# Transposes, splits and index matmuls of a mixture-of-experts stage, moved into the products before them

## The chip, the cores and the metric

One core of a Trainium2 chip runs the whole program. The metric is the time of one execution on the device, in microseconds; the number for a kernel is the median of its runs. Profiles come from one execution taken by the hardware profiler.

## What is computed

The reference is two blocks over 1024 tokens of 1024 channels. The first has a Fourier branch, a bidirectional mLSTM branch and a mixture of 16 experts, in which each expert chooses its 128 best tokens; the second is a hybrid mixer. The change touches the experts alone:

```python
aff = jax.nn.softmax(h @ w_router, axis=-1)
vals, idx = lax.top_k(jnp.swapaxes(aff, 1, 2), 128)
xs = h[idx]
hid = jax.nn.silu(xs @ w_gate) * (xs @ w_up)
y = (hid @ w_down) * vals[..., None]
x = x + ga2 * jnp.zeros_like(h).at[idx].add(y)
```

All weights are float32, 1024 x 1024 for each of the three products of an expert, and each is read once from device memory.

## The kernel before, in words

Matrix products are made in a fast reduced float format. To keep float32 accuracy, each operand is split into a high part (a copy in that format) and a low part (the rest); a product is then three matmuls, high by high, high by low and low by high (`mm3`, line 354).

**Weights.** Weights are loaded in units of 1 MB, two steps of 128 input channels each, on SyncE's queue. Each step is split: ScalarE copies the high part, VectorE subtracts to get the low part (`_split`, line 234). `prefetch` (line 263) keeps up to six split steps, five ahead of the one in use, and fills all other free memory with raw units. Memory is 25 slots of 8 KB a partition; a raw unit, a split step, an expert's tokens and a transposed operand take one slot each. `slot` (line 182) gives out the free slot that is done with first, by a plan of the engines' times that the kernel keeps while it is built; a load or a write into a slot waits until the slot's last use has ended.

**One expert.** The tokens of expert e are gathered by POOL from device memory by a list of indices (`gather`, line 1670), 128 tokens on partitions. `transp` (line 1676) turns them: TensorE transposes eight 128 x 128 blocks into two banks of PSUM, ScalarE copies the high part and VectorE subtracts for the low part. `prod` (line 1690) makes one product of 128 x 1024: 8 steps of 2 halves of 3 matmuls, 48 in all, over two banks. Gate goes through SiLU on ScalarE, is multiplied by up on VectorE, turned by `transp` again, and multiplied by down. VectorE scales the result and POOL adds it to the tokens in device memory with an indirect scatter.

**Indices.** `index` (line 1657) finds the tokens of an expert: one row of a 48-row table of running counts is spread over 128 partitions by a matmul with a one-hot column (two matmuls of 48 rows, one for each half of the 1024 tokens), and VectorE counts, over each half, how many running counts are not above its slot number. The table is filled once, before the first expert.

**Order.** The instructions are issued in an order written out by hand. Round e of the loop (line 1727) is: up of e; multiply by the gate of e; transpose the tokens of e+1; gather e+2; build the indices 2e+3 and 2e+4 (so that all are there after e = 6); gate of e+1, and its SiLU; transpose the hidden values of e; down of e; scale; scatter. Each engine works off its own instructions in this order. There are four PSUM banks for products (`pm`) and four for all else (`pa`). All instructions pass through one helper, so that the profile gives line 67 for each.

Of the kernel before, what the change touches and what calls it, by code (L numbers as in the profile page):

```python
# [9 lines left out]
FT = mybir.dt.float32  # L10
# [19 lines left out]
# columns of the host-laid-out vector tile  # L30
C_C, C_CC, C_G1, C_G2, C_GF, C_BA = 0, 8, 16, 24, 32, 40
C_WC = 56                 # 9 taps x 8 blocks
C_CA = C_WC + 72          # 3 taps x 2
C_DW = C_CA + 6           # 31 taps x 2
# [5 lines left out]
# constant table columns  # L40
# [13 lines left out]
class Queue:  # L54
    """an engine of the core that books what is given to it in the plan"""
# [15 lines left out]
class Plan:  # L71
    """the core with its engines, and about when each of them gets to what it has been given, in microseconds:
    background work is given to an engine when its operands are about to be there"""
# [79 lines left out]
class Kern:  # L153
# [27 lines left out]
    # ---- memory  # L181
    def slot(self, dt=FT, name="t"):
        """8 KB a partition"""
        s = Slot()
        assert self.free_slots, "out of slots: " + " ".join(sorted(x.c for x in self.live.values()))
        s.i, s.c = self.free_slots.pop(self.pick()), name
        self.live[s.i] = s
        self.n += 1
        s.t = self.sp.tile([128, SLOT], dt, tag=f"s{s.i}", name=f"{name}_{self.n}")
        self.tags[s.i] = s.t.tensor.tag  # L190
        return s

    def pick(self):
        """the slot that is done with first"""
        def at(i):
            tag = self.tags.get(i)
            return max((d[tag, b][0] for d in (self.nc.wrote, self.nc.read) for b in range(17) if (tag, b) in d), default=0.0)
        f = [at(i) for i in self.free_slots]
        return f.index(min(f))
# [14 lines left out]
    # ---- weights: raw units of 8 KB a partition, split into two hi/lo pairs  # L214
# [75 lines left out]
    def get_raw(self):  # L290
        """next unit that is used as it comes"""
# [12 lines left out]
    # ---- background work  # L304
# [3 lines left out]
    def pump(self, us=1.3):  # L308
        """lets background work of about us microseconds be issued in each lane"""
# [9 lines left out]
    def until(self, *aps):  # L319
        """waits in the background until the tensor engine would not wait for these"""  # L320
# [3 lines left out]
    def soon(self, *aps):  # L324
        """near the end of the routing: the vector engine sorts until these are there"""
# [5 lines left out]
    def calm(self, eng="DVE", lead=None):  # L331
        """waits in the background until the engine has not much to do"""
# [20 lines left out]
    # ---- arithmetic helpers  # L353
    def mm3(self, ps, w, h, start, stop):
        """ps += w^T h for pairs (hi, lo) of exact splits"""
# [5 lines left out]
    def inv_sqrt(self, out, v, scale, eps):  # L361
        """out = 1 / sqrt(v * scale + eps)"""
# [8 lines left out]
    def bcast(self, src, n):  # L371
        """[128, n] read of n contiguous DRAM floats, the same for all partitions"""
        return bass.AP(tensor=src.tensor, offset=src.offset, ap=[[0, 128], [1, n]])

    # =====================================================================
# [6 lines left out]
    def consts(self):  # L382
# [36 lines left out]
        self.slotc = self.kc[:, K_SL:K_SL + 1]  # L419
        nc.vector.tensor_copy(self.one[0:32], self.idn[0:32, 0:16])  # L420
# [10 lines left out]
    # ---------------------------------------------------------------------  # L431
    def start(self):
# [50 lines left out]
        # shift and scale of x and of the context: silu(c) @ w_ada[:, :2048], channels on partitions  # L483
# [146 lines left out]
    # ---------------------------------------------------------------------  # L630
    def chan(self, w, hs, evac, cols=128, order=None):
        """one block of output channels on partitions; hs: per 512 tokens the (hi, lo) of each k"""
# [21 lines left out]
    def tok(self, wa, wb, h, t, evac):  # L654
        """token tile t of a 256-column unit; wa, wb: k 0..3 and 4..7"""
# [11 lines left out]
    # ---------------------------------------------------------------------  # L667
    def load_wg(self):
# [6 lines left out]
        # kinds: input gate, forget gate of the two directions  # L675
# [7 lines left out]
    def gates(self, ps, T, m0, gcol, kinds, after):  # L683
        """ps: banks of raw gates [100, T]; leaves per-token columns in gcol and calls after(views)"""
# [36 lines left out]
        # chunk-local inclusive sums of the log forget gates, running from either end  # L721
# [38 lines left out]
    # ---------------------------------------------------------------------  # L760
    def conv(self, raw, out, blk, rows, tail):
        """depthwise 3x3 (SAME) of one channel block over a grid of rows x L/rows"""
# [28 lines left out]
    # ---------------------------------------------------------------------  # L791
    def ctx_pass(self):
# [12 lines left out]
        def after(v):  # L805
            # the states that the context leaves
# [62 lines left out]
    # ---------------------------------------------------------------------  # L869
    def px_front(self):  # L870
# [14 lines left out]
        # q, k  # L885
# [34 lines left out]
    # ---------------------------------------------------------------------  # L920
    def fourier_in(self):
# [38 lines left out]
        def fold(tmp, src, sgn, i, P, dst, n):  # L960
            """src [P, 4 x 128] in PSUM: channels c and 128 - c of each group together, then hi/lo"""
# [43 lines left out]
    def fourier(self):  # L1005
# [6 lines left out]
        # spectrum over the tokens k = 0..512: P even, Q odd  # L1012
        P, Q, Px = self.slot(FR, "P"), None, self.slot(FR, "Px")

        def pq(s, t, x):
            """hi, lo of chunk x of tile t"""
# [31 lines left out]
        # channel transform folded into w_fourier, then the product, half of the output channels at a time  # L1048
# [58 lines left out]
    # ---------------------------------------------------------------------  # L1107
# [24 lines left out]
    def ada_step(self, n):  # L1132
        """one unit of the other modulation vectors: products summed over the partitions at the end"""
# [35 lines left out]
    def mlstm(self, h):  # L1169
        """both directions of head h; leaves h^T (head dim on partitions) in the place of k"""  # L1170
        nc = self.nc
        q, k, v = self.qv[h], self.kv[h], self.vv[h]
        t1 = self.slot(FT, "ml")            # k by token | output by token
        kt = t1.t[:, 0:1024].rearrange("p (c d) -> p c d", c=8)
        hh = t1.t[:, 1024:2048].rearrange("p (c d) -> p c d", c=8)
        Wt = self.slot(FT, "mw")            # weights of both directions [s, (c, j)]
        W = [Wt.t[:, d * 1024:(d + 1) * 1024] for d in range(2)]
        X = self.slot(FT, "bd")             # cum - m of both directions, then the decays, then the decayed q
# [36 lines left out]
        ws = self.slot(FT, "wv")            # weighted values | states  # L1215
# [46 lines left out]
        for c4 in range(2):  # L1262
# [4 lines left out]
            # the halves of sigmoid(x) = (1 + tanh(x / 2)) / 2 go with the other factor  # L1267
# [6 lines left out]
    # ---------------------------------------------------------------------  # L1274
    def branch1(self):
        """first branch gate times the Fourier branch; output gate; second branch"""
# [95 lines left out]
    # ---------------------------------------------------------------------  # L1372
    def router(self):
        """router on the unscaled tokens: logits = rstd * (x1 . (A2 w)) + sh2 . w"""
# [26 lines left out]
    def out_proj(self):  # L1401
        """x1 = x + ga1 * (merged @ w_out); h2; router; running top-k"""
# [91 lines left out]
    def memory(self, kv):  # L1494
        """keys (channels on partitions) and values (rows on partitions) of the memory"""
# [12 lines left out]
    def post(self, n, ps, x, h2, hT, t):  # L1508
        """half n of the columns: x1, its squares, x1^T"""
# [18 lines left out]
    def route(self, t, x, h2, hT):  # L1528
        """the tokens for the experts, with their affinities behind them"""
# [41 lines left out]
        # sorted lists of the 128 largest: even tiles on rows 0-15, odd ones on rows 32-47  # L1571
# [12 lines left out]
    def clean(self, bufs, dst, d):  # L1584
        """sorts bitonic lists of 2 d, largest first"""
# [11 lines left out]
    def join(self, new):  # L1597
        """the 128 largest of two sorted lists, sorted"""
# [8 lines left out]
    def top(self, cur, dst, tmp):  # L1607
        """128 values of each row sorted, largest first: two halves, then both"""
# [19 lines left out]
    # ---------------------------------------------------------------------  # L1628
    def experts(self, r2, kv):
        nc = self.nc  # L1630
        AT = self.AT
        # threshold: the 128th largest affinity of each expert, from the two sorted lists
# [6 lines left out]
        # rows 0-15 count the affinities above it; rows 32-47 those equal to it, as far as there is room  # L1639
        cs, cm = self.slot(FT, "cs"), self.slot(FR, "cm")  # L1640
        sel, run = cs.t[0:48, 0:1024], cs.t[0:48, 1024:2048]
# [15 lines left out]
        def index(e):  # L1657
            """tokens of expert e in the order of their index: slot s has cum <= s before it"""
            f = self.idf[:, 2 * (e % 2):2 * (e % 2) + 2]
            for n in range(2):  # L1660
                ps = self.bank("pa")
                nc.tensor.matmul(ps, self.one[0:48, e:e + 1].to_broadcast([48, 128]), cum[:, n * 512:(n + 1) * 512],
# [13 lines left out]
        def transp(src):  # L1676
            o = self.slot(FR, "xT")
            hi, lo = (o.t[:, i * 1024:(i + 1) * 1024] for i in range(2))
            for k4 in range(2):
                p = self.bank("pa", (4, 128))  # L1680
                for k in range(4):
                    kk = k4 * 4 + k
                    nc.tensor.transpose(p[:, k], src[:, kk * 128:(kk + 1) * 128], self.idn)
                pf = p.rearrange("p a b -> p (a b)")
                c = slice(k4 * 512, (k4 + 1) * 512)
                nc.scalar.activation(hi[:, c], pf, AF.Copy)
                nc.vector.tensor_sub(lo[:, c], pf, hi[:, c].bitcast(FT))
            return o

        def prod(o):  # L1690
            pss = [self.bank("pm") for _ in range(2)]
            for k in range(8):
# [5 lines left out]
                self.done(w)  # L1698
            return pss

# [19 lines left out]
        xT = {0: transp(xs[0].t)}  # L1720
# [6 lines left out]
        for e in range(NE):  # L1727
# [5 lines left out]
            pu = prod(xT[e])  # L1733
# [4 lines left out]
            if e + 1 < NE:  # L1738
                xT[e + 1] = transp(xs[e + 1].t)
                if e + 2 < NE:  # L1740
                    gather(e + 2)
                for i in range(2 * e + 3, min(2 * e + 5, NE)):
                    index(i)
                if 2 * e + 4 == NE:
                    self.free(cm)
                g[e + 1] = silu(e + 1, prod(xT[e + 1]))
            hT = transp(g.pop(e))
            if e == NE - 1:
                # the last rows are added to the tokens on chip, too: one-hot rows of their places
# [561 lines left out]
```

## Time and profile before

| | us |
|---|---|
| median of 3 runs | 2015.81 |
| lowest and highest run | 2014.33, 2016.72 |
| span of the profiled execution | 2013.5 |

The profiled execution has no time of its own beside its span, from the first instruction to the last; the span is 2.3 us under the median of the runs. The experts take from about 880 to 1505 us of it. Busy times over the span are 1901.8 us (94%) on TensorE, 1430.7 (71%) on VectorE, 893.2 (44%) on ScalarE and 207.4 (10%) on POOL. In the profile PE is TensorE, PEld its weight loads, DVE is VectorE, ACT is ScalarE, SP is SyncE. `w` is a split weight step, `raw` a loaded unit, `xs` the tokens of an expert (with its gate values behind them), `xT` a transposed operand, `cm` the table of running counts, `x1d` the tokens in device memory. A matmul's own duration overlaps that of the next, so distances of starts say more than durations.

### The profile page before, as it was taken

Reading aid. Unit: us, or ns where it says so; the run is one execution under the profiler, and the core shown is the slowest. Engines: PE = TensorE matmul, PEld = TensorE weight load, DVE = VectorE, ACT = ScalarE, POOL = GpSimd, SP = SyncE. Lnnn points to the kernel's source line nnn. Section 1 sums busy time; section 2 is a strip of 40 time slices with the busy share of each in tenths; the row PEclk is TensorE's granted clock in tenths of the full one; section 3 lists DMA queues with packets and bytes.
Section 4 is the critical chain, followed back from the end, with each engine's and each line's share of the span. In section 5 each row is a group of like instructions: output and inputs, shape, how many; then the busy total and the mean of one; then the engine's idle time right before and its main releaser. Section 6 shows DMA issues by size and latency. Waiting matters only on the chain.

```text
span 2013.5 us, 23979 instructions
## 1 busy us (share of the span) xinstructions
PE 1901.8 (94%) x9258; PEld 1523.0 (76%) x9258; DVE 1430.7 (71%) x2110; ACT 893.2 (44%) x1256; POOL 207.4 (10%) x186
## 2 busy tenths in 40 slices
PE   7899999999999999769999999999998999999997
PEld 3687888888877777557777777777777987678786
DVE  7797775556644547779889988888884787663544
ACT  5623432222322242346677677777765223433300
POOL 1300000000000034531001001101010000000011
PEclk9899999999999999879999999999999999999999
DMA  8101126434234343668989999999961101011322
GB/s 344 63 26 33 32 105 231 157 126 147 74 126 141 121 155 128 251 255 314 338 316 358 341 386 367 359 361 370 364 244 45 53 21 42 27 43 42 107 82 74
DMA packets 92317, 361.03 MB, mean 179 GB/s; under 512 B 9742, under 2 KB 10775, under 8 KB 85932
## 3 DMA queue, kind: packets, MB, share of 16 engines
q1 hardware_dynamic: 78156, 318.17, 42.0%
q0 software_dynamic: 9952, 35.42, 5.8%
q10 hardware_dynamic: 4096, 5.91, 0.9%
q8 instruction: 73, 1.20, 0.3%
q14 instruction: 40, 0.33, 0.0%
HBM read 329.96 MB, written 29.52 MB: 179 GB/s over the span
## 4 chain that ended last, share of the span: by engine, by line
PE 82%; DVE 10%; ACT 4%; issue 2%; DMA 2%; POOL 0%; ACTq 0%; POOLq 0%; DVEq 0%; SPq 0%
PE pm L67 73%; PE pa L67 9%; DVE w L67 2%; DVE tk L67 2%; ACT w L67 1%; DVE xs L67 1%; DMA bd<-gd 1%; DVE gt L67 1%; DVE mw L67 1%; DVE xT L67 1%; DVE tx L67 1%; ACT xT L67 0%; DMA wgr<-in_w_g 0%; DVE tm L67 0%; ACT gt L67 0%
## 5 line engine op out<-in xcount | busy, mean ns | idle before, releaser
L67 DVE TENSOR_TENSOR w<-raw,w 128x1024 fp32r<-128x1024 f32 (+1 forms) x496 | 590.6, 1226 | 104.7 <-ACT w L67 94.4
L67 ACT ACTIVATE w<-raw 128x1024 fp32r<-128x1024 f32 (+1 forms) x504 | 515.8, 1055 | 143.1 <-PE pm L67 125.1
L67 PE MATMUL pm<-w,xT 128*128 128x512 f32 x2304 | 556.0, 400 | 19.8 <-DVE xT L67 8.4
L67 PEld LDWEIGHTS pm<-w,xT 128*128 128x128 f32 x2304 | 434.2, 190 | 135.6 <-DVE xT L67 19.2
L67 PE MATMUL pm<-hT,w 128*128 128x512 f32 x1536 | 382.6, 400 | 0.0
L67 PEld LDWEIGHTS pm<-hT,w 128*128 128x128 f32 x1536 | 283.6, 190 | 60.4 <-issue 1.7
L67 PE MATMUL pm<-x,w 128*128 128x512 f32 x1152 | 281.0, 399 | 0.0
L67 PEld LDWEIGHTS pm<-x,w 128*128 128x128 f32 x1152 | 213.9, 188 | 53.8 <-issue 8.4
L67 PE MATMUL pm<-w,hh 128*128 128x512 f32 x480 | 111.3, 393 | 0.9 <-DVE w L67 0.9
L67 PEld LDWEIGHTS pm<-w,hh 128*128 128x128 f32 x480 | 90.2, 188 | 21.9 <-DVE w L67 1.3
L67 PE MATMUL pm<-w,mg 128*128 128x512 f32 x384 | 97.3, 402 | 0.0
L67 PEld LDWEIGHTS pm<-w,mg 128*128 128x128 f32 x384 | 69.5, 188 | 16.1 <-issue 1.5
L67 POOL DMA_INDIRECT x1d<-xs,idx x16 | 36.4, 2273 | 426.1 <-DVE xs L67 374.3
L67 DVE SCALAR_TENSOR_TENSOR qk<-raw,cols,qk 128x945 f32<-128x945 f32 (+2 forms) x64 | 78.0, 1219 | 1.3
L67 DVE SCALAR_TENSOR_TENSOR dg<-da,cols,dg 128x1023 f32<-128x1023 f32 (+29 forms) x60 | 76.0, 1267 | 1.6
L67 DVE TENSOR_TENSOR xT<-pa,xT 128x512 fp32r<-128x512 f32 x64 | 41.2, 684 | 25.5 <-ACT xT L67 25.5
L67 ACT ACTIVATE b<-pm 128x512 f32<-128x512 f32 x32 | 19.1, 598 | 66.4 <-PE pm L67 63.5
L67 POOL TENSOR_SCALAR sm<-sm 128x1 f32<-128x1 f32 x16 | 11.2, 702 | 362.5 <-DVE sm L67 361.7
L67 PE MATMUL pm<-om,w 128*128 128x512 f32 x192 | 46.6, 404 | 1.7 <-ACT om L67 0.9
L67 PEld LDWEIGHTS pm<-w,hT 128*128 128x128 f32 x384 | 46.0, 189 | 2.2 <-ACT w L67 0.9
L67 PE MATMUL pm<-w,hT 128*128 128x256 f32 x384 | 46.8, 283 | 0.2 <-DVE w L67 0.2
L67 PEld LDWEIGHTS pm<-w,x 128*128 128x128 f32 x384 | 45.7, 189 | 0.1
(364 smaller groups left out, 2070.8 us busy)
## 6 DMA issues: line engine op xcount, KB each, us to landing
raw<-in_w_gate SPq DMA_DIRECT2D x64, 1024.0 KB, 9.1
raw<-in_w_down SPq DMA_DIRECT2D x64, 1024.0 KB, 6.0
raw<-in_w_up SPq DMA_DIRECT2D x63, 1024.0 KB, 12.8
raw<-in_w_in SPq DMA_DIRECT2D x34, 1024.0 KB, 5.7
raw<-in_w_ada SPq DMA_DIRECT2D x24, 1024.0 KB, 7.8
raw<-in_w_out SPq DMA_DIRECT2D x9, 1024.0 KB, 4.9
b<-yd SPq DMA_DIRECT2D x16, 512.0 KB, 3.6
h2d<-tx POOLq DMA_DIRECT2D x8, 520.0 KB, 3.1
```

Source lines behind the costliest of these rows:

```text
L67: return f(*a, **kw)
```

## The change

Comments are taken out all over the file. What else changes:

- `transp` makes one half (four blocks) at a time, into a slot that the caller gives.
- `prod` takes a function that is called after each of the 8 steps. In up of e it takes a slot after step 2 (the third) and transposes the tokens of e+1, four blocks after step 2 and four after step 4. In gate of e+1 it does the same with the hidden values of e. In down of e it builds index 2e+3 after step 2 and index 2e+4 after step 5.
- For the first tokens and for the hidden values of the last expert the transposes stay outside the products.
- Index matmuls go over 128 rows; the rows of the table beyond 48 are cleared by POOL, those of the one-hot tile by VectorE.
- The table's slot is freed after down of e = 6 and not before gate of 7.

```diff
+        nc.vector.memset(self.one.bitcast(FT), 0.0)
...
         cs, cm = self.slot(FT, "cs"), self.slot(FR, "cm")
+        nc.gpsimd.memset(cm.t[:, 0:1024].bitcast(FT), 0.0)
...
-                nc.tensor.matmul(ps, self.one[0:48, e:e + 1].to_broadcast([48, 128]), cum[:, n * 512:(n + 1) * 512],
+                nc.tensor.matmul(ps, self.one[:, e:e + 1].to_broadcast([128, 128]), cm.t[:, n * 512:(n + 1) * 512],
                                  start=True, stop=True)
...
-        def transp(src):
-            o = self.slot(FR, "xT")
+        def transp(src, o, k4):
             hi, lo = (o.t[:, i * 1024:(i + 1) * 1024] for i in range(2))
-            for k4 in range(2):
-                p = self.bank("pa", (4, 128))
...
+            p = self.bank("pa", (4, 128))
+            for k in range(4):
+                kk = k4 * 4 + k
+                nc.tensor.transpose(p[:, k], src[:, kk * 128:(kk + 1) * 128], self.idn)
+            pf = p.rearrange("p a b -> p (a b)")
+            c = slice(k4 * 512, (k4 + 1) * 512)
+            nc.scalar.activation(hi[:, c], pf, AF.Copy)
+            nc.vector.tensor_sub(lo[:, c], pf, hi[:, c].bitcast(FT))
...
-        def prod(o):
+        def prod(o, between=None):
...
                 self.done(w)
+                if between:
+                    between(k)
             return pss
+
+        def turned(src, dst, key):
+            def between(k):
+                if k == 2:
+                    dst[key] = self.slot(FR, "xT")
+                if k in (2, 4):
+                    transp(src, dst[key], k // 2 - 1)
+            return between
...
-            pu = prod(xT[e])
+            pu = prod(xT[e], turned(xs[e + 1].t, xT, e + 1) if e + 1 < NE else None)
...
             if e + 1 < NE:
-                xT[e + 1] = transp(xs[e + 1].t)
                 if e + 2 < NE:
                     gather(e + 2)
-                for i in range(2 * e + 3, min(2 * e + 5, NE)):
-                    index(i)
-                if 2 * e + 4 == NE:
-                    self.free(cm)
-                g[e + 1] = silu(e + 1, prod(xT[e + 1]))
-            hT = transp(g.pop(e))
+                g[e + 1] = silu(e + 1, prod(xT[e + 1], turned(g[e], hT, e)))
             if e == NE - 1:
+                hT[e] = self.slot(FR, "xT")
+                for k4 in range(2):
+                    transp(g[e], hT[e], k4)
...
-            pd = prod(hT)
-            self.free(hT)
+            def next_indices(k):
+                i = 2 * e + 3 + (k - 2) // 3
+                if k in (2, 5) and i < NE:
+                    index(i)
+            pd = prod(hT[e], next_indices)
+            self.free(hT.pop(e))
+            if 2 * e + 4 == NE:
+                self.free(cm)
```

## Rows read from the trace of the kernel before

**Rows 1.** The page, part 4: the chain that ended last, by line.
```profile
PE pm L67 73%; PE pa L67 9%; DVE w L67 2%; DVE tk L67 2%; ACT w L67 1%; DVE xs L67 1%; DMA bd<-gd 1%; DVE gt L67 1%; DVE mw L67 1%; DVE xT L67 1%; DVE tx L67 1%; ACT xT L67 0%; DMA wgr<-in_w_g 0%; DVE tm L67 0%; ACT gt L67 0%
```
**Rows 2.** Timeline of POOL: scatters (start us, us, instruction, count, idle before and releaser).
```profile
940.94 2.36 POOL L67 DMA_INDIRECT x1d<-xs,idx  x1 [27.40 <-DVE xs L67]
...
1062.93 2.31 POOL L67 DMA_INDIRECT x1d<-xs,idx  x1 [28.99 <-DVE xs L67]
...
1101.86 2.31 POOL L67 DMA_INDIRECT x1d<-xs,idx  x1 [27.22 <-DVE xs L67]
...
1142.52 2.31 POOL L67 DMA_INDIRECT x1d<-xs,idx  x1 [28.89 <-DVE xs L67]
...
1180.05 2.31 POOL L67 DMA_INDIRECT x1d<-xs,idx  x1 [25.88 <-DMA raw<-in_w_down]
...
1442.50 2.31 POOL L67 DMA_INDIRECT x1d<-xs,idx  x1 [25.85 <-DVE xs L67]
```
**Rows 3.** Timeline of TensorE in the round that begins at 1255.11.
```profile
1264.78 1.04 PE L67 MATMUL pa<-kc,xs 128*128 128x128 f32 x8
...
1266.06 0.72 PE L67 MATMUL pm<-w,xT 128*128 128x512 f32 x2 [0.25 <-ACT xT L67]
...
1267.77 10.86 PE L67 MATMUL pm<-w,xT 128*128 128x512 f32 x46 [0.99 <-DVE xT L67]
...
1278.47 1.04 PE L67 MATMUL pa<-kc,xs 128*128 128x128 f32 x8
...
1279.81 22.60 PE L67 MATMUL pm<-w,xT 128*128 128x512 f32 x96 [0.30 <-ACT xT L67]
...
1280.54 21.45 PEld L67 LDWEIGHTS pm<-w,xT 128*128 128x128 f32 x94 [0.43 <-DVE xT L67]
```
**Rows 4.** Timeline of TensorE in the round that begins at 981.59.
```profile
991.30 1.03 PE L67 MATMUL pa<-kc,xs 128*128 128x128 f32 x8
...
992.26 0.73 PE L67 MATMUL pa<-cm,one 48*128 48x512 f32 x2
...
994.30 1.10 PE L67 MATMUL pa<-cm,one 48*128 48x512 f32 x2 [1.30 <-DVE xT L67]
...
994.90 0.18 PEld L67 LDWEIGHTS pa<-cm,one 48*128 48x128 f32 x1 [0.42 <-DVE xT L67]
...
995.33 12.91 PE L67 MATMUL pm<-w,xT 128*128 128x512 f32 x48
```
**Rows 5.** Windows: busy us by engine (instructions), granted clock, DMA share, GB/s.
```profile
1180.05:1442.50 262.45, 251.76 (x1121) 200.15 (x1120) 233.60 (x225) 195.65 (x210) 27.13 (x14) 1.00 0.98 364
996.30:999.70 3.40, 3.40 (x9) 2.63 (x9) 3.37 (x8) 1.06 (x1) 0.00 (x0) 0.50 1.02 412
999.80:1003.20 3.40, 3.40 (x16) 2.80 (x15) 2.27 (x3) 1.85 (x2) 0.00 (x0) 1.00 0.81 308
1022.20:1062.90 40.70, 39.00 (x165) 30.46 (x164) 36.29 (x43) 27.73 (x30) 3.39 (x2) 0.96 0.92 338
1230.00:1235.00 5.00, 4.72 (x20) 3.87 (x21) 4.35 (x6) 3.48 (x4) 0.00 (x0) 1.00 1.03 420
```
**Rows 6.** Timeline: the first gather on POOL, and VectorE's multiply by the gate.
```profile
873.08 1.05 POOL L67 DMA_INDIRECT xs<-h2d,idx  x1 [15.09 <-issue]
...
992.37 1.28 DVE L67 TENSOR_TENSOR xs<-xs,pm 128x512 f32<-128x512 f32 x2
```
**Rows 7.** The instructions of the tile xs on POOL: landing of gathers and scatters.
```profile
DMA to landing us min/median/max: 4.3/9.4/11.5
```
**Rows 8.** Groups by form, 941 to 1101.86 (VectorE) and whole run (POOL): busy, mean ns, idle before.
```profile
L67 DVE TENSOR_TENSOR w<-raw,w 128x1024 fp32r<-128x1024 f32 x97 | 115.1, 1221 | 12.7 <-ACT w L67 11.1
...
L67 DVE TENSOR_TENSOR xT<-pa,xT 128x512 fp32r<-128x512 f32 x16 | 10.3, 683 | 2.7 <-ACT xT L67 2.7
...
L67 POOL MEMSET tk<- 48x1024 f32 x1 | 1.0, 961 | 28.2 <-PE pm L67 28.2
```
**Rows 9.** Waits of SyncE's queue, 1180 to 1442.5 (total us, times, longest us).
```profile
SPq L67 <- DVE w L67: 186.0, 62, 7.3
```

More of the change, by code (lines that the diff above doesn't have):

```diff
@@ L1674, in gather @@
             xs[e] = s
-        def transp(src):
-            o = self.slot(FR, "xT")
+        def transp(src, o, k4):
             hi, lo = (o.t[:, i * 1024:(i + 1) * 1024] for i in range(2))
-            for k4 in range(2):
-                p = self.bank("pa", (4, 128))
[L1681 to L1688, printed above, removed]
-        def prod(o):
+            p = self.bank("pa", (4, 128))
[7 more added lines that the diff above has]
+        def prod(o, between=None):
             pss = [self.bank("pm") for _ in range(2)]
@@ L1719, in experts @@
             self.done(w)
-        xT = {0: transp(xs[0].t)}
+        xT, hT = {0: self.slot(FR, "xT")}, {}
+        for k4 in range(2):
+            transp(xs[0].t, xT[0], k4)
         index(2)
@@ L1738, in experts @@
             if e + 1 < NE:
-                xT[e + 1] = transp(xs[e + 1].t)
                 if e + 2 < NE:
                     gather(e + 2)
-                for i in range(2 * e + 3, min(2 * e + 5, NE)):
-                    index(i)
-                if 2 * e + 4 == NE:
-                    self.free(cm)
-                g[e + 1] = silu(e + 1, prod(xT[e + 1]))
-            hT = transp(g.pop(e))
+                g[e + 1] = silu(e + 1, prod(xT[e + 1], turned(g[e], hT, e)))
             if e == NE - 1:
+                hT[e] = self.slot(FR, "xT")
+                for k4 in range(2):
+                    transp(g[e], hT[e], k4)
                 x2 = [self.slot(FT, "x2") for _ in range(4)]
```

## The prediction

> **What bounds the kernel now.** I read the page first, then the scatters that end each expert, then TensorE's instructions of one late and one early expert, then windows over the same stretches. In the chain of waits 73% of the span are matmuls into the product banks [rows 1], so what TensorE does between two products counts directly. The scatter of expert e is issued when its down product is done, so the distance of two scatters is one round (up of e, gate of e+1, down of e). There are two kinds of round [rows 2]: with two indices built, 201.58 us for e = 1 to 5, one of 38.93 and four of 40.66 on average; and without, 262.45 us for the seven from e = 7 on, 37.49 each.
>
> A round has 144 product matmuls. In an unbroken stretch 94 weight loads start within 21.45 us [rows 3], 0.2286 us apart: 32.9 us a round. The rest of a late round is its two transpose stretches: from the first transpose to where the matmuls run on (two lone matmuls, 0.46 us, taken off) 1264.78 to 1267.77 is 2.53 us, and 1278.47 to 1280.54 is 1.61 us [rows 3]. 32.9 + 4.14 = 37.0; the last 0.4 us is slow re-entry, 0.1 us on the second matmul after each of four breaks. In an early round the first stretch runs from 991.30 to 995.33, 4.03 us, for the third index matmul stands 1.30 us behind a bank that VectorE still reads [rows 4]; and then the granted clock is 0.50 (1.2 GHz) from 996.30 to 999.70, with 9 matmuls started where the next 3.40 us, at 2.4 GHz, have 16 [rows 5]: 7 x 0.2286 = 1.6 us. 32.9 + 4.03 + 1.61 + 1.6 + 0.4 = 40.5, near the 40.66; the round of 38.93 is 1.7 shorter, one without such a fall. So there are to be had 4.1 us of a late round (2.1 of it transposes that stay) and some 7.2 of an early one.
>
> Two limits lie close below. VectorE is busy 36.29 us of an early round and 233.60 / 7 = 33.4 of a late one. The DMA engines show a share of 0.98 over the late rounds, and 1.03 where they are saturated: 37.49 x 0.98 / 1.03 = 35.7 us a round is what the loads need [rows 5].
>
> **The change, part by part.** *Transposes.* Eight in a row twice a round become four after step 2 and four after step 4, in up (the next tokens) and in gate (the hidden values). Their operands are early: the product of gate and up is ready 1.28 us after VectorE starts on it at up's end [rows 6], and the first transposes stand 18 matmuls (4.1 us) behind that end; a gather or scatter lands 11.5 us after its issue at most [rows 7], and its tokens are wanted more than a gate and a down product later. So the waits for the transposed parts go: these are due a whole product later. What stays is 4 x 0.11 us a group (eight take 1.03, of which 0.27 is the length of the last [rows 4]) and the re-entry. The nearest rows: the last transpose starts at 992.06, the next matmul at 992.26, 0.20 later, thus 0.09 over a transpose's own spacing [rows 4]; plus the 0.1 on the second matmul: 0.63 a group, 2.5 for four groups. Late round by TensorE: 32.9 + 2.5 = 35.4. The loads need 35.7, and I take 35.9, a little over both. Bounds: with no re-entry at all 35.7, by the loads; with the 0.30 us wait of the second stretch [rows 3] at each of four breaks as well, 36.6.
>
> *Index matmuls.* Four of them (two indices) go in pairs after steps 2 and 5 of down, with four banks to rotate, so the bank wait (1.30 us) goes. A pair costs at least two spacings, 0.46 us, and at most what it costs now without a wait, 0.43 a matmul (994.90 to 995.33) [rows 4], 0.87. Two pairs: 0.9 to 1.7; I take 1.3, the middle, because over 128 rows they look more like the product's own matmuls (0.2286), yet each pair is again a break. The Trainium skill (TensorE: Matmul & The Clock Gate, section Why this matters for your kernels) says that a single matmul over few rows takes the time of one over all 128. By it alone the wider form gives nothing back, and the term would be the 1.7 of today, 0.4 us more in five rounds. Early round by TensorE: 35.4 + 1.3 = 36.7; VectorE needs 36.3; I take 37.1, because two engines that both fill the round and feed each other will not meet without a gap.
>
> *The half clock.* It follows the stretch with the bank wait in four of five rounds; the seven late rounds stand at 1.00 [rows 5], though their breaks reach 0.99 us of idle [rows 3]. The new breaks have no wait, so I count the 1.6 us as gone.
>
> *ScalarE and VectorE* issue the same copies and subtractions, only earlier and between the weight splits, which run five steps ahead (6.9 us against some 2.3 us of work for one); this lead covers the 1.3 to 1.8 us that each group puts in front of them. Without that cover the splits are late and TensorE waits: the first rival. *Slots.* A second transposed tile is held from step 2 of up and of gate, so one raw buffer fewer is free there. SyncE's loads wait for VectorE to release a buffer, 186.0 us over the late rounds in 62 waits [rows 9]: the buffers are full, so one less costs nothing until loads run late (the second rival). *POOL.* The clearing of the 128-row tile stands ahead of the first gather. Over 48 rows one takes 0.96 us [rows 8]; POOL is idle for 15.09 us before that gather [rows 6], whose index comes from this tile: nothing. Gathers and scatters keep their order; indices now come after the gather of e+2, which uses ones built a round earlier. The clearing of the 16-column tile is one small VectorE instruction at the start: nothing.
>
> **Sum.** e = 1 to 5: 201.58 - 5 x 37.1 = 16.1. Seven late rounds: 262.45 - 7 x 35.9 = 11.1. e = 6 (one index; 1142.52 to 1180.05, 37.53 [rows 2], to 36.5): 1.0. e = 14, as a late one: 1.6. e = 0 has the same two stretches, counted as the round of 38.93: 1.8. Together 31.6 us. The last expert keeps its transposes outside. The profiled span is 2013.5 us, 2.3 under the median of 2015.81, and what lies around it is taken as unchanged: 1982 for the profile's span, 1984 for the median. With the low bounds (35.7 late and VectorE's 36.3 early) the gain is 39, with the high ones (36.6 and 36.6 + 1.7 = 38.3) 18: 1977 to 1998.
>
> **Rivals.** *VectorE takes over.* An early round needs 36.29 us of it, and it waits besides: in four early rounds 12.7 us before splits and 2.7 before transposed parts [rows 8], 3.85 a round. If half of this stays because transposes, parts and splits now alternate, the early round is 38.2; that takes 5.5 from five rounds and 2 from e = 0 and 6: 1992. For it: its share. Against it: most of the waits are for ScalarE, which itself waits for TensorE to free a weight slot, and TensorE would be quicker. If all of the waits stay, because a transpose group holds the product behind it as the bank wait held the gate product [rows 4], the rounds remain as they are, 2014 to 2016: the wait has moved and the change does nothing. The Trainium skill (the same page, section Step-by-step: what each phase is for) says that weight loads alone are pulled ahead and matmuls stay in program order, by which that last case is possible.
>
> *The loads take over.* One raw buffer less, and the share has little room. If 0.98 is all that they reach, a round needs 36.7 and eight late rounds gain 6.4 us less: 1991. Against it: the buffers are full now.
>
> *Slower: the half clock.* Each product with transposes now has two breaks. If the clock fell once in gate and once in up, a round would lose 3.2 us: late 39.1, early 40.3. Sum: eight late rounds 1.6 us longer, e = 6 and e = 0 2.2 and 1.4, e = 1 to 5 unchanged: 2032. It decides from 31.6 / 1.6 = 20 falls in the stage; by the sums above there are four now. For it: the fall stood behind transposes and index matmuls. Against it: the late rounds have the same transposes and more idle than the new order, and no fall [rows 5]. The Trainium skill (the same page, section Part 4: PE-mode transpose) says that the high clock does not engage for transposes, which would speak for this rival; the late rounds at 1.00 do not bear it out.
>
> **How the numbers follow.** Forecast 0.66; VectorE by half 0.14 and loads 0.08; waits moved and nothing gained 0.06; half clock 0.06. The first three are faster (0.88); of the next two I give 0.05 to the same and 0.07 to slower. The range holds the forecast, the two cases about 1991 and a VectorE case half as bad again: 1976 to 2003. A measurement of this kernel tells about 0.2%, 4 us, from no change.
>
> **What would show it.** Scatters some 37 us apart early and 36 late; no granted clock of 0.5 between the scatters at e = 0 and e = 6; waits for transposed parts gone from the first product matmuls; transposes in groups of four with the next product matmul some 0.2 us behind the last; a DMA share near its saturated value in late rounds. I am wrong if TensorE waits for VectorE at a transpose group or for a split, if loads land after their split is due, or if the clock falls inside the products.

## The result and the profile after

The changed kernel takes 1969.09 us (1967.26 to 1970.82, 4 runs) against 2016.26 of the kernel before in the same runs: a ratio of 0.9769, interval 0.9758 to 0.9781. The direction was right and the size was not: 47 us were gained where 32 were forecast, and 1969 lies under the range that began at 1976. The profiled spans are 1965.9 and 2013.5 us, 47.6 apart; these are compared below.

The scatters in the changed kernel (timeline of POOL), to be held against [rows 2]:

```profile
938.77 4.63 POOL L67 DMA_INDIRECT x1d<-xs,idx  x1 [25.58 <-DVE xs L67]
...
1118.59 2.31 POOL L67 DMA_INDIRECT x1d<-xs,idx  x1 [26.00 <-DVE xs L67]
...
1153.09 2.31 POOL L67 DMA_INDIRECT x1d<-xs,idx  x1 [24.53 <-DVE xs L67]
...
1397.84 2.31 POOL L67 DMA_INDIRECT x1d<-xs,idx  x1 [22.96 <-DVE xs L67]
...
1431.69 10.25 POOL L67 DMA_INDIRECT x1d<-xs,idx  x1 [31.55 <-DVE xs L67]
```

Differences of these starts give the account:

| rounds | before, us | after, us | gain | forecast |
|---|---|---|---|---|
| up to the scatter of e = 0 | 940.94 | 938.77 | 2.2 | 1.8 |
| e = 1 to 5 | 201.58 (40.32 each) | 179.82 (35.96) | 21.8 | 16.1 |
| e = 6 | 37.53 | 34.50 | 3.0 | 1.0 |
| e = 7 to 13 | 262.45 (37.49) | 244.75 (34.96) | 17.7 | 11.1 |
| e = 14 | 37.41 | 33.85 | 3.6 | 1.6 |
| from there to the end | 533.6 | 534.2 | -0.6 | 0 |

Windows over the same two kinds of round, late and early (columns as in [rows 5]; the engines are TensorE, its weight loads, VectorE, ScalarE, POOL):

```profile
1153.09:1397.84 244.75, 244.75 (x1121) 200.32 (x1120) 229.49 (x225) 190.81 (x210) 26.12 (x15) 1.00 1.03 395
938.77:1118.59 179.82, 179.82 (x821) 146.89 (x820) 177.25 (x211) 136.85 (x151) 19.89 (x10) 1.00 1.01 380
```

TensorE is busy for all of both stretches, where [rows 5] had 251.76 of 262.45 and 39.00 of 40.70. The clock stands at 1.00 in both. VectorE has 177.25 / 5 = 35.5 us in an early round of 35.96, and the DMA share is 1.01 early and 1.03 late.

TensorE's timeline in a late round, at up's first and second group and the matmuls behind them (answers [rows 3]):

```profile
1189.56 0.60 PE L67 MATMUL pa<-kc,xs 128*128 128x128 f32 x4
1189.92 3.03 PE L67 MATMUL pm<-w,xT 128*128 128x512 f32 x12
1192.79 0.60 PE L67 MATMUL pa<-kc,xs 128*128 128x128 f32 x4
```

Four transposes start at 1189.56, 0.11 apart, so the last starts at 1189.89; the next product matmul starts at 1189.92, 0.03 later. The prediction had 0.20 there. And a down product of an early round, with its two pairs of index matmuls (answers [rows 4]):

```profile
999.12 0.63 PE L67 MATMUL pa<-cm,one 128*128 128x512 f32 x2
999.59 4.30 PE L67 MATMUL pm<-w,xT 128*128 128x512 f32 x18
1003.72 0.63 PE L67 MATMUL pa<-cm,one 128*128 128x512 f32 x2
1004.19 7.13 PE L67 MATMUL pm<-w,xT 128*128 128x512 f32 x30
```

Two index matmuls take 0.47 us, 0.235 each, the spacing of the product's own. Last, what TensorE waited for before its product matmuls in the whole run (instructions of the tile xT on PE):

```profile
its engine sat idle before it (us, times) until:
  POOL w L67: 4.6, 3
  ACT w L67: 1.3, 1
```

The waits for the transposed parts, such as the 0.99 and 0.30 us of [rows 3], are gone. The 5.9 us left lie in the gate product of the first expert, before any group stands in a product.

### The profile page after: what moved, and what is told of

Read it like the earlier page. It is cut to its first block, busy times and chain, and to the rows that moved or that the text cites. A ratio compares the mean times of both kernels' runs of the same rounds, so it can differ in the third digit from the quotient of the medians.

```text
span 1965.9 us, 23992 instructions
## 1 busy us (share of the span) xinstructions
PE 1876.9 (95%) x9258; PEld 1516.3 (77%) x9258; DVE 1421.8 (72%) x2111; ACT 884.9 (45%) x1256; POOL 219.0 (11%) x187
## 4 chain that ended last, share of the span: by engine, by line
PE 87%; DVE 7%; ACT 2%; issue 1%; DMA 1%; POOL 1%; ACTq 0%; POOLq 0%; DVEq 0%; SPq 0%
PE pm L67 76%; PE pa L67 11%; DVE tk L67 2%; DVE gt L67 1%; DVE tx L67 1%; DMA bd<-gd 1%; DVE w L67 1%; POOL w L67 1%; DVE mw L67 0%; DMA wgr<-in_w_g 0%; DVE tm L67 0%; ACT gt L67 0%; DMA b<-yd 0%; ACT x L67 0%; DVE b L67 0%
## 5 line engine op out<-in xcount | busy, mean ns | idle before, releaser
L67 ACT ACTIVATE w<-raw 128x1024 fp32r<-128x1024 f32 (+1 forms) x504 | 510.3, 1051 | 107.4 <-PE pm L67 99.9
L67 PEld LDWEIGHTS pm<-w,xT 128*128 128x128 f32 x2304 | 428.9, 188 | 102.2 <-POOL w L67 6.3
L67 POOL DMA_INDIRECT x1d<-xs,idx x16 | 46.6, 2912 | 385.6 <-DVE xs L67 378.0
L67 ACT ACTIVATE xT<-pa 128x512 fp32r<-128x512 f32 x64 | 37.7, 591 | 30.1 <-PE pa L67 29.9
```

The lines of the kernel that those rows point to most:

```text
L67: return f(*a, **kw)
```

## The experiments

### The two halves of the change, each alone

*Index matmuls alone*: the kernel before, with the index matmuls over 128 rows inside the down products and the transposes between the products as they were.

```diff
-                for i in range(2 * e + 3, min(2 * e + 5, NE)):
-                    index(i)
...
-            pd = prod(hT)
+            pd = prod(hT, next_indices)
```

> The kernel before with the index matmuls over 128 rows inside the down products, transposes as before. If the parts simply add: early rounds become late ones plus four spacings, 37.5 + 0.9 = 38.4 us, no half clock: 5 x 1.9 + 0.5 = 10 us less, 2006. If VectorE's counting in down delays the splits: 2012 to 2016.

It took 2004.24 us against 2015.46, ratio 0.9942 (0.9926 to 0.9957). The window over e = 1 to 5 is 192.50 us, 38.5 a round, at a clock of 1.00:

```profile
942.70:1135.20 192.50, 184.90 (x822) 146.73 (x821) 178.85 (x211) 139.16 (x151) 16.98 (x11) 1.00 0.96 355
```

So that half takes 11 us off alone, as the parts added up.

*Transposes alone*: the changed kernel, with the index matmuls at their old place between up and gate and over 48 rows.

```diff
+                for i in range(2 * e + 3, min(2 * e + 5, NE)):
+                    index(i)
                 g[e + 1] = silu(e + 1, prod(xT[e + 1], turned(g[e], hT, e)))
...
-            pd = prod(hT[e], next_indices)
+            pd = prod(hT[e])
```

> The changed kernel with the index matmuls of 48 rows back between up and gate; the transposes stay inside the products. Late rounds as in the changed kernel, 35.0 us. Early rounds: with the transposes elsewhere their banks are free and the 1.30 us wait is gone: 34.9 + four index matmuls at 0.34 to 0.43 = 36.3 to 36.6 us; 2 us in all above the changed kernel, 1971. If index matmuls between the products bring the half clock by themselves: 1.6 us more in some four rounds, 1977 to 1979.

1970.30 us, ratio 0.9780 (0.9765 to 0.9795). TensorE's timeline in an early round:

```profile
983.70 1.19 PE L67 MATMUL pa<-cm,one 48*128 48x512 f32 x4
984.82 4.36 PE L67 MATMUL pm<-w,xT 128*128 128x512 f32 x18
```

All four index matmuls run on without a wait (1.12 us to the next product matmul), and the window over e = 1 to 5 has 181.70 us, 36.3 a round, with a clock of 1.00:

```profile
938.20:1119.90 181.70, 181.70 (x822) 146.06 (x821) 176.64 (x211) 138.60 (x150) 23.52 (x11) 1.00 1.01 376
```

The transposes alone bring 45 us of the 47. With the index part alone worth 11, the two halves overlap: moving either ends the bank wait, for it was the transposes that held two of the four banks while four index matmuls asked for theirs.

### What brought the half clock, and what the 128 rows do

*128 rows alone*: the kernel before with only the width of the index matmuls changed (and the two clears that the wider form needs).

```diff
-                nc.tensor.matmul(ps, self.one[0:48, e:e + 1].to_broadcast([48, 128]), cum[:, n * 512:(n + 1) * 512],
+                nc.tensor.matmul(ps, self.one[:, e:e + 1].to_broadcast([128, 128]), cm.t[:, n * 512:(n + 1) * 512],
```

> The kernel before with index matmuls over 128 rows at their old place between up and gate. If the width brings the half clock and the slow index matmuls: four falls of 1.6 us and 26 times 0.1 to 0.2 us go, 2005 to 2010. If the bank wait brings them: 2014 to 2017, with four stretches at 0.50 still there.

2010.02 us, ratio 0.9973 (0.9962 to 0.9984): the time is at the edge of what was expected if the width did it, but in the trace falls are there, as expected if the wait does it. The bank wait stands, and three of the four falls do. TensorE's timeline first, then a window on the stretch behind it:

```profile
1027.66 1.03 PE L67 MATMUL pa<-kc,xs 128*128 128x128 f32 x8
1028.45 0.72 PE L67 MATMUL pa<-cm,one 128*128 128x512 f32 x2
1030.63 1.26 PE L67 MATMUL pa<-cm,one 128*128 128x512 f32 x2 [1.47 <-DVE xT L67]
```

```profile
1031.40:1034.80 3.40, 3.40 (x9) 2.66 (x10) 3.33 (x11) 0.31 (x1) 0.00 (x0) 0.50 1.04 424
```

So the width alone does not keep the clock up. The run with the transposes alone has 48 rows, no wait and no fall; the run here has 128 rows, the wait and falls. The falls come with the wait, though not with each: in the kernel before and in this one all of the rounds e = 1 to 5 have it, and four and three of them a fall. In the runs in which the index matmuls or the transposes are moved, no fall stands between the scatters of e = 0 and e = 13, but for the run without low parts below, where TensorE waits for loads. What decides between two rounds with the same wait stays open. So does whether the width makes falls rarer. In the trace it shortens a round without a fall by 0.1 us at most (38.93 and 38.81 us against 38.93) and one with a fall by some 0.2, which is less than the 5 us of the median. But the profiled execution took 2013.48 us and has the lowest mean clock of the seven, 0.979 where the others have 0.980 to 0.983, so the faster ones may have had fewer falls. The first row carries a second thing: eight transposes from 1027.66 put the last start at 1028.42, and the index matmul follows at 1028.45, 0.03 later. In the kernel before it was 0.20 with 48 rows [rows 4]. So 0.17 of that 0.20 was the price of a 48-row matmul behind a 128-row one.

*48 rows inside down*: the changed kernel with the line above turned back.

```diff
-                nc.tensor.matmul(ps, self.one[:, e:e + 1].to_broadcast([128, 128]), cm.t[:, n * 512:(n + 1) * 512],
+                nc.tensor.matmul(ps, self.one[0:48, e:e + 1].to_broadcast([48, 128]), cum[:, n * 512:(n + 1) * 512],
```

> The changed kernel with index matmuls of 48 rows again, still inside the down products. If the width matters (an index matmul over 48 rows costs 0.34 to 0.43 us as in the kernel before, over 128 rows 0.23): 26 matmuls of e = 0 to 6 cost 0.11 to 0.20 us more, 3 to 5 us, and with the half clock back behind some of them up to 6 more: 1972 to 1980. If only the place matters: 1969, with 0.23 us from an index matmul to the next.

1973.07 us, ratio 0.9794 (0.9780 to 0.9807), against 0.9769 (0.9758 to 0.9781) of the changed kernel; the two intervals just overlap. In the traces the late rounds are the same 244.75 us, and five early ones take 183.75 us against 179.82, 0.79 more each.

```profile
1000.76 0.72 PE L67 MATMUL pa<-cm,one 48*128 48x512 f32 x2
1001.42 4.40 PE L67 MATMUL pm<-w,xT 128*128 128x512 f32 x18
```

A pair now takes 0.66 us and not 0.47, and another 0.2 is lost on the matmuls beside it. The granted clock stays at 1.00. The sentence of the Trainium skill that the prediction weighed (TensorE: Matmul & The Clock Gate, section Why this matters for your kernels: few rows take the time of all) does not hold between wider neighbours here: the change of width costs some 0.4 us a pair. It is the change that costs and not the few rows: in the run with the transposes alone four 48-row matmuls stand in a row, and an early round has 0.4 us over the changed kernel's and not 0.8 (36.35 against 35.96 us).

### What a group of transposes costs

*One group of eight* in place of two of four, all after step 2:

```diff
                 if k == 2:
                     dst[key] = self.slot(FR, "xT")
-                if k in (2, 4):
-                    transp(src, dst[key], k // 2 - 1)
+                    for k4 in range(2):
+                        transp(src, dst[key], k4)
```

> The changed kernel with all eight transposes after step 2 and none after step 4. If each group costs 0.19 us of re-entry over its transposes, as the prediction had it, 30 groups less are 5.7 us less: 1963. If transposes with operands at hand cost their own 0.11 us alone: 1969, within 1 us.

1969.68 us, ratio 0.9767 (0.9754 to 0.9781): no difference. In the trace eight transposes and the way back take 0.79 us, twice the 0.36 and a little:

```profile
1187.64 1.03 PE L67 MATMUL pa<-kc,xs 128*128 128x128 f32 x8
1188.43 11.38 PE L67 MATMUL pm<-w,xT 128*128 128x512 f32 x48
```

The early rounds are the same 179.82 us, the late ones 0.12 us shorter each, with two breaks fewer. The price is for each transpose, and hardly for the break.

*Groups after steps 0 and 1*, where the hidden values are hardly ready:

```diff
-                if k == 2:
+                if k == 0:
                     dst[key] = self.slot(FR, "xT")
-                if k in (2, 4):
-                    transp(src, dst[key], k // 2 - 1)
+                if k in (0, 1):
+                    transp(src, dst[key], k)
```

> The changed kernel with the groups after steps 0 and 1 instead of 2 and 4. The hidden values of a round are ready some 2.5 to 3.1 us behind up's end, and the first group in gate then stands 1.4 us behind it. If matmuls wait in order: TensorE stands 1.1 to 1.5 us at the first group of each gate, 15 times: 17 to 22 us more, 1986 to 1991. If something takes up the wait (the split steps run ahead): 1969 to 1973.

1977.01 us, ratio 0.9807 (0.9792 to 0.9822): 8 us more than the change, less than half of what a wait in order was expected to cost. The window over the five early rounds, 184.42 us, has TensorE idle for 3.75 us, and each round is 0.92 longer:

```profile
936.95:1121.37 184.42, 180.67 (x823) 146.51 (x822) 176.72 (x211) 136.88 (x151) 21.98 (x10) 1.00 1.01 371
```

The late rounds are 0.44 longer. TensorE's timeline at the first group of a gate, in an early and in a late round:

```profile
984.53 0.66 PE L67 MATMUL pa<-kc,xs 128*128 128x128 f32 x4 [0.65 <-DVE xs L67]
...
1203.76 0.65 PE L67 MATMUL pa<-kc,xs 128*128 128x128 f32 x4 [0.25 <-DVE xs L67]
```

Matmuls wait in order, as expected, but VectorE gets to the multiply sooner than I took from the changed kernel's trace, where it starts 1.7 us behind up's end: here 1.3 to 1.5 us early and 0.9 to 1.0 late. And the first four blocks wait for the first half of the multiply alone. The cover of 4.1 us that steps 2 and 4 give is real and is needed in part.

### Which limit holds the rounds now

*Without low parts*: the subtractions for the low parts of the expert weights and the matmuls with them are left out, all loads stay.

```diff
-        (nc.gpsimd if u in self.pool_lo else nc.vector).tensor_sub(lo, src, hi.bitcast(FT))
+        if not self.lo_out[0] <= u < self.lo_out[1]:
+            (nc.gpsimd if u in self.pool_lo else nc.vector).tensor_sub(lo, src, hi.bitcast(FT))
...
-                    self.mm3(pss[n], lh, (w[1][:, 0, n * 512:(n + 1) * 512], w[2][:, 0, n * 512:(n + 1) * 512]),
-                             k == 0, k == 7)
+                    wh = w[1][:, 0, n * 512:(n + 1) * 512]
+                    nc.tensor.matmul(pss[n], lh[0], wh, start=k == 0, stop=False)
+                    nc.tensor.matmul(pss[n], lh[1], wh, start=False, stop=k == 7)
```

> The changed kernel without the low parts of the expert weights: VectorE's subtractions for them and one matmul in three are left out (the products lose accuracy), all loads stay. TensorE then needs 96 x 0.23 + 1.8 = 23.9 us a round, VectorE some 6, ScalarE 29. If the loads need 35.7 us a round, as the prediction had it, the late rounds come out at 35.7, no shorter than now. If they can do the bytes at the best rate seen, 13.7 MB at 420 GB/s, they come out at 32.6.

A single run of 1932.79 us. With a third of the product work gone the late rounds are 34.6 us, between the two numbers. The window goes from the scatter of e = 6 to that of e = 13; below it are waits between 1150 and 1380 us (total us, times, longest):

```profile
1116.05:1358.30 242.25, 196.19 (x786) 131.15 (x785) 37.56 (x56) 188.00 (x210) 17.98 (x14) 0.97 1.03 396
```

```profile
PE pm L67 <- ACT w L67: 42.0, 50, 3.1
ACT w L67 <- DMA raw<-in_w_gate: 33.4, 21, 2.7
```

No engine is full, TensorE waits for ScalarE's splits, ScalarE for loads, and the share is 1.03: this is what the loads need, 242.25 / 7 = 34.6 us a round. My 35.7 was too long and 32.6, at the best rate of a few microseconds, too short.

*Half of the loads*: every unit loads its first half, and both of its steps are split from that half, so that each second step of the weights does not enter the result.

```diff
-        self.loader.dma_start(self._raw_view(u), self.units[u][0])
+        v, src = self._raw_view(u), self.units[u][0]
+        if self.half[0] <= u < self.half[1]:
+            v, src = v[:, 0:1], src[:, 0:1]
+        self.loader.dma_start(v, src)
...
-            src = raw[:, j:j + 1, :]
+            j2 = 0 if self.half[0] <= u < self.half[1] else j
+            src = raw[:, j2:j2 + 1, :]
```

> The changed kernel with half of each expert weight unit loaded; both of its steps are split from the half that is there, so each second step of weights is left out of the result and all engine work stays. If TensorE alone sets the changed kernel's rounds (144 x 0.2295 + 4 x 0.44 = 34.8 us late, 35.8 early), the rounds stay at 34.9 and 35.9 and the stage gains under 3 us: 1966 to 1969. If the loads, whose share is 1.03 there, hold the late rounds, these fall by more than 0.5 us: under 1965.

1968.85 us, ratio 0.9767 (0.9749 to 0.9785), and the seven late rounds are 244.75 us, the same to the second decimal, at a share of 0.66:

```profile
1153.02:1397.77 244.75, 244.75 (x1121) 200.32 (x1120) 229.48 (x225) 190.77 (x210) 26.09 (x15) 1.00 0.66 213
```

The loads do not hold the changed kernel, although their share reads 1.03. What is left is TensorE, which waits for nothing in these rounds; no run took work off it alone.

*Each count twice* on VectorE:

```diff
-                nc.vector.tensor_scalar(rg.t[:, 1024 + n * 512:1536 + n * 512], ps, self.slotc, None, op0=OP.is_le, op1=OP.add,
-                                        accum_out=f[:, n:n + 1])
+                for _ in range(2):
+                    nc.vector.tensor_scalar(rg.t[:, 1024 + n * 512:1536 + n * 512], ps, self.slotc, None, op0=OP.is_le, op1=OP.add,
+                                            accum_out=f[:, n:n + 1])
```

> The changed kernel in which VectorE does each count of an index twice (the second overwrites the first with the same number): four more instructions of 0.67 to 0.74 us in each early round, 2.7 to 3.0 us. If VectorE is right below the bound there (35.4 us busy of 35.96), early rounds rise to some 38.2 and six rounds make 13 us: 1982. If it has room for them: 1969.

1982.45 us, ratio 0.9835 (0.9817 to 0.9853). The early rounds are 38.4 us, as two scatters on POOL's timeline show:

```profile
939.94 2.36 POOL L67 DMA_INDIRECT x1d<-xs,idx  x1 [27.61 <-DVE xs L67]
978.35 2.31 POOL L67 DMA_INDIRECT x1d<-xs,idx  x1 [31.55 <-DVE xs L67]
```

In the window over five of them VectorE (the third engine of the row) is busy 191.00 of 192.06 us:

```profile
939.94:1132.00 192.06, 183.61 (x824) 146.70 (x824) 191.00 (x251) 136.28 (x151) 23.34 (x11) 1.00 0.99 358
```

Four counts of 0.67 us make 2.7; 191.00 / 5 - 2.7 = 35.5 us is what VectorE needs in an early round. In the changed kernel it has half a microsecond to spare. Its weight splits run on there, as its timeline in an early round shows:

```profile
974.35 3.49 DVE L67 TENSOR_TENSOR w<-raw,w 128x1024 fp32r<-128x1024 f32 x3
...
978.38 1.23 DVE L67 TENSOR_TENSOR w<-raw,w 128x1024 fp32r<-128x1024 f32 x1
```

## Why the prediction was right or wrong, point by point

The mechanism held. What failed are three terms of the sum, all too large: the price of a transpose group, what the loads need, and what an early round needs of VectorE, with the gap added to it. The last two stood as floors under the range as well: 35.7 us late and 36.3 early, where 34.96 and 35.96 came.

- **What was lost between products** [rows 3 to 5]: right. The waits for transposed parts, the bank wait and the half clock are all gone. The order of the losses is right too: a round of e = 1 to 5 gains the most.
- **The price of a transpose group**: the first wrong term. I took 0.63 us: 0.44 for four transposes, 0.09 over the spacing from 992.06 to 992.26 [rows 4], and 0.1 on the second matmul. The first addition came from a row with something else in it. The 0.09 belongs to the 48-row matmul that followed, not to leaving the transposes: behind transposes both a 128-row index matmul and a product matmul start 0.03 us later, 0.08 sooner than another transpose would. That 0.08 pays for the slow second matmul, which is real. So four transposes cost 4 x 0.11 = 0.44 and nothing more, 1.8 us a round where I had 2.5: 11 us in 15 rounds. It was my low bound.
- **The loads' need**: the second wrong term. I scaled the share, 37.49 x 0.98 / 1.03 = 35.7, as if a byte took the same share in a full queue as in one that at times runs dry. It does not: 0.98 stood beside 364 GB/s [rows 5], 1.03 beside 395 and, with half of the loads, 0.66 beside 213. The loads need 34.6 us (the run without low parts). With the first term right and 35.7 kept, I should still have forecast 35.9 for the late rounds. The measured 34.96 is TensorE's: 32.9 + 1.8 = 34.7, and 0.3 of spread in the spacing. 0.9 us in seven rounds is 6.6 us of the miss.
- **Index matmuls**: 1.3 us taken, 0.94 measured (four at 0.235), the low bound. With 48 rows they cost 0.79 more, 1.7: the high bound. I took the middle for the wider form; the width made the whole difference between the bounds.
- **VectorE's need** of 36.3 us in an early round: 35.5. Its busy time in the kernel before was that of instructions of which many stood alone: of the 120 weight splits of e = 1 to 5, 62 had no idle time before them, and in the changed kernel 105. Splits that run on overlap and take less (three in 3.49 us, one alone in 1.23). I added 0.4 us over TensorE's 36.7 for the two working hand in hand, and nothing was to be added: TensorE is never idle. The early round is 35.96 and not 37.1, which is 5.7 us in five rounds; TensorE's own terms, 32.9 + 1.8 + 0.9, make 35.6 of it.
- **The half clock**: right that it goes. The runs above show it behind the bank wait and gone with it, and not what spared the rounds that had the wait and no fall.
- **The rivals**: the first two fell, both close by: VectorE has 0.5 us to spare early, the loads 0.3 late. The clock did not fall inside the products; as the rival's counter said, the rounds stand at 1.00. The Trainium skill (the same page, section Part 4: PE-mode transpose) says that the high clock does not engage for transposes; that brought no loss here.
- **The edges**: the gains at e = 6 and 14 were 2.0 over the forecast each, since a scatter also waits for VectorE's queue, and how far that lags differs from one kind of round to the next. In the kernel before each of these scatters starts some 1.2 us behind the end of its down product (1.1 at e = 14); in the changed kernel 3.5 us early, 2.6 late and 1.3 at e = 14. Over all rounds this nearly cancels. So the 2.2 us of the first row, near the forecast of 1.8, are luck: the products began 1.6 us sooner and took 2.9 less, and the lag took 2.3 back. The end of the stage lost 0.6 us. Why the scatter of e = 14 stood 10.25 us on POOL stays open.

## What to carry to other kernels

Work that stands between two dense products and waits for its own results costs more than itself: here the wait, and at times the half clock behind it. Put it into a product some steps behind the point where its operand is ready, and count its own spacing alone. A price of re-entry must be read from a row in which nothing else changes (here the width of the next matmul did), and a busy share from a stretch with gaps is no floor for one without: what limits next is found by taking work off one engine at a time.

## What was not expected of the hardware

Two matmuls over 48 rows between matmuls over 128 cost some 0.4 us more than two over 128 rows (0.79 us for two pairs), without any wait in the trace; four in a row cost the same 0.4 us once. A product matmul starts 0.03 us behind a float32 transpose, although transposes start 0.11 us apart, and the next one is then 0.08 us late. The DMA share read 1.03 in a stretch whose time did not change by 0.01 us when half of the loads were left out.
